# The end of a Strassen down product: its stores, its residual buffers and its early loads

## The chip, the cores and the metric

The kernel runs on one core of one Trainium2 chip. The metric is the device time in microseconds; three runs gave 2256.93 to 2257.66 us, median 2257.65 us.

## The reference, cut to what matters

A trunk of two layers on 1024 rows of width 1024, in float32. Layer 0 has an attention mixer, layer 1 a recurrent one. Each mixer and each FFN is a sub-layer with a norm ahead of it and one behind it:

```python
h = rmsnorm(x, norm_ffn_pre[layer])
f = (silu(h @ w_gate) * (h @ w_up)) @ w_down      # 1024 -> 2816 -> 1024
x = x + rmsnorm(f, norm_ffn_post[layer])
```

The part that is changed is the last product (`w_down`) and the residual addition behind it, once for each layer. Behind layer 0 the recurrent mixer follows, behind layer 1 the output.

## The kernel before, in words

Every matrix product is made in three passes on TensorE, high x high, high x low and low x high, so each float32 operand is split: a cast on ScalarE (line 584) and a subtraction on VectorE (line 585) give the two parts. The gate, up and down products are Strassen products with seven block products instead of eight.

`down` makes seven products out of 11 steps j each (2816 is 22 x 128, so a step j is a pair of row blocks of `w_down`). A step has 4 token blocks x 3 matmuls (lines 589 to 591, 128x128 by 128x512). The left operands (A11, S2, S3, S1, A22, S4, A12) were written to DRAM by the gate and up stage; the right operands are blocks of `w_down` or sums of them, kept in `t` tiles (one for each j, in a pool at the right end of the memory) until the fifth product. Each product's operands arrive through `raw` (three buffers), go through `split` into `w` (eight buffers, left) and `wb` (four buffers, right) and are used by TensorE in the order of j.

With the fifth product four of the eight row blocks are finished ("r = 1"), and `norm(1, a)` can be made for the four a: load x (line 181), multiply by the gain (line 212), square sum on ScalarE (line 164), rstd in one-column operations on GpSimd (lines 166 to 168), add (line 215), store (line 217, two DMAs of 64 rows each). Then come the sixth product (`p3`, left S4, loads at lines 681 and 682), which adds to the other four blocks, the eleven B21 blocks (line 691) and, one a after the other, the seventh product: three loads of A12 (through `load`, line 181), their splits (lines 700 and 701), 33 matmuls, the addition (line 706) and `norm(0, a)`. In layer 0 there is a `sink`: the norm goes on into the next mixer's norm (`pre_norm`, a second rstd and eight transposes on TensorE, line 197, whose results are split in lines 57 and 58). In layer 1 `sink` is None.

The order of each engine's instructions is set ahead of the run by a planner: it walks a timeline of its own and gives an engine next the first instruction in program order that this timeline finds ready. On the chip each engine, and each queue of DMA issues, then keeps that order and waits where something is late. `load` adds one rule: its DMA is issued behind the instruction `self.mark`, here the last load of the fifth product. All DMAs of this part are issued by SyncE, but for the second half of each store in layer 1, which ScalarE issues.

Of the kernel before, what the change touches and what calls it, by code (L numbers as in the profile page):

```python
# [8 lines left out]
F32 = mybir.dt.float32  # L9
# [6 lines left out]
P = 128  # L16
S = 1024
D = 1024
# [80 lines left out]
class Trunk:  # L99
# [98 lines left out]
            pst.append(ps.rearrange("p (a b) -> p a b", a=4))  # L198
        sink.take(t, pst, h, pool)

    def post_norm(self, ms, mg, x_src, x_dst, t, gpost, sink, pool):


        nc = self.nc
        x = pool.tile([P, D], F32, tag="nx", bufs=2, name=self.uid("x"))
        for d, s in rows(t, x_src):
            self.load(x[d, :], s)
        junk = pool.tile([P, D // len(ms)], BF16, tag="junk", bufs=1, name=self.uid("junk"))
        if mg is ms[0][1]:
            rs = self.rstd(pool, [m for _, m in ms], junk)  # L210
        for c, m in ms:
            nc.vector.tensor_tensor(mg[:, c], m, gpost[:, c], op=ALU.mult)
        if mg is not ms[0][1]:
            rs = self.rstd(pool, [m for _, m in ms], junk)
        nc.vector.scalar_tensor_tensor(x, mg, rs, x, op0=ALU.mult, op1=ALU.add)
        for k, (d, s) in enumerate(rows(t, x_dst)):
            (nc.scalar if k and sink is None else nc.sync).dma_start(s, x[d, :])
        if sink is not None:
            self.pre_norm(pool, x, mg, None, sink, t, self.psum_t)

# [187 lines left out]
    def out_product(self, ap, aT, w, x_src, x_dst, gpost_v, sink, kts):  # L408

        nc = self.nc  # L410
        wv = [w[kt * P:(kt + 1) * P, :].rearrange("p (a b) -> p a b", a=2) for kt in range(KT)]

        def act(kt, t0, n, pool, bufs, tag="act"):
            a = pool.tile([P, 384], F32, tag=tag, bufs=bufs, name=self.uid("act"))[:, :n * P]
            nc.sync.dma_start(a, aT[kt][:, t0 * P:(t0 + n) * P])
            return a

        def matmuls(ps, passes, first, last):

            for n in range(2):  # L420
                for i, (x, y) in enumerate(passes):
                    nc.tensor.matmul(ps[n], x, y[:, n, :], start=first and i == 0,
                                     stop=last and i == len(passes) - 1)

        def norm(t, ps):
            mg = ap.tile([P, D], F32, tag="mg", bufs=3, name=self.uid("mg"))
            ms = [(slice(i * 512, (i + 1) * 512), p) for i, p in enumerate(ps)]
            self.post_norm(ms, mg, x_src, x_dst, t, gpost, sink, ap)

        gpost = None  # L430
        for t0 in (0, 3):
            pst = [[self.psum() for _ in range(2)] for _ in range(3)]
            for kt in kts:
                pool, bufs = (self.apool, 1) if t0 == 0 and kt == kts[0] else (ap, 3)
                a = act(kt, t0, 3, pool, bufs)
                wh, wl = self.split(wv[kt], 2, 512)
                ah, al = (pool.tile([P, 384], F32R, tag=n, bufs=bufs, name=self.uid(n)) for n in ("ah", "al"))
                nc.scalar.copy(ah, a)
                nc.vector.tensor_tensor(al, a, ah.bitcast(F32), op=ALU.subtract)
                for t in range(3):  # L440
                    tok = slice(t * P, (t + 1) * P)
                    matmuls(pst[t], [(ah[:, tok], wh), (ah[:, tok], wl), (al[:, tok], wh)],
                            kt == kts[0], kt == kts[-1])
            if gpost is None:
                gpost = self.gain(ap, "gpost", gpost_v)
            for t in range(3):
                norm(t0 + t, pst[t])

        rows, acts = [], []
        for i, kt in enumerate(kts):  # L450
            raw = self.main.tile([P, 2, 512], F32, tag="w", bufs=8, name=self.uid("raw"))
            nc.sync.dma_start(raw, wv[kt])
            rows.append(raw)
            acts.append(act(kt, 6, 2, ap, 3, ("act", "ah", "al")[i % 3]))
        for t in range(2):
            ps = [self.psum() for _ in range(2)]
            for i in range(KT):
                matmuls(ps, [(acts[i][:, t * P:(t + 1) * P], rows[i])], i == 0, i == KT - 1)
            norm(6 + t, ps)
# [109 lines left out]
    def down(self, l, gO, x_src, x_dst, make_sink):  # L569
# [4 lines left out]
        nc, io = self.nc, self.io  # L574
# [4 lines left out]
        def block(j, row, c0=0, n=D):  # L579
            return w[(2 * j + row) * P:(2 * j + row + 1) * P, c0:c0 + n]  # L580
# [23 lines left out]
        with self.pool(f"d{l}") as ap:  # L604
# [3 lines left out]
            with self.pool(f"da{l}", "right") as da:  # L608
# [56 lines left out]
                    tt(n[:, hi], ps, n[:, lo], op=ALU.add)  # L665
                for n, ps in zip(m2, product(p4)):
                    tt(n[:, lo], n[:, lo], ps, op=ALU.subtract)
            with make_sink() as sink:
                def norm(r, a, m):
                    ms, mg = [(slice(0, D), m)], m  # L670
                    if r == 0 and sink is None:
                        ms = [(c, m[:, c]) for c in (hi, lo)]
                        mg = ap.tile([P, D], F32, tag="mg", bufs=1, name=self.uid("mg"))
                    self.post_norm(ms, mg, x_src, x_dst, (r, a), gpost, sink, ap)

                for a in range(4):
                    norm(1, a, m2[a])

                def p3(j):
                    r = main.tile([P, 2, 512], F32, tag="raw", bufs=3, name=self.uid("raw"))  # L680
                    nc.sync.dma_start(r[:, 0], gO["S4"][j])
                    nc.sync.dma_start(r[:, 1], block(j, 1, 512, 512))
                    return split(main, "w", 8, r[:, 0]), split(ap, "wb", 4, r[:, 1])

                for m, ps in zip(m1, product(p3)):
                    tt(m[:, hi], ps, m[:, hi], op=ALU.add)
                b21 = []
                for j in range(NP):
                    if j % 2 == 0:
                        r = main.tile([P, 2, 512], F32, tag="raw", bufs=3, name=self.uid("raw"))  # L690
                    nc.sync.dma_start(r[:, j % 2], block(j, 1, 0, 512))
                    b21.append(split(*((main, "w", 8) if j < 6 else (ap, "wc", 5)), r[:, j % 2]))
                for a in range(4):
                    ops = []
                    for j in range(0, NP, 4):
                        n = min(4, NP - j)
                        r = ap.tile([P, 4, P], F32, tag="act", bufs=2, name=self.uid("act"))[:, :n]
                        self.load(r, gO["A12"][:, j:j + n, a * P:(a + 1) * P])
                        t = ap.tile([P, 2, 4, P], F32R, tag="wb", bufs=4, name=self.uid("o"))
                        nc.scalar.copy(t[:, 0, :n], r)  # L700
                        tt(t[:, 1, :n], r, t[:, 0, :n].bitcast(F32), op=ALU.subtract)  # L701
                        ops += [(t[:, 0, i], t[:, 1, i]) for i in range(n)]
# [243 lines left out]
```

## Time and profile before

| | |
|---|---|
| median of the runs | 2257.65 us |
| profiled execution, own time | 2262.01 us |
| its span, first to last instruction | 2260.2 us |
| TensorE busy | 2201.2 us, 97% of the span |
| VectorE busy | 1551.9 us, 69% |
| ScalarE busy | 1149.1 us, 51% |
| GpSimd busy | 168.3 us, 7% |
| moved by DMA | 273.63 MB, mean 121 GB/s |

The shares are means over stages with different limits, so a change in one stage is read from that stage's own windows. In the rows PE is TensorE, PEld its weight loads, DVE VectorE, ACT ScalarE, POOL GpSimd and SP SyncE; a q behind the name is the engine's queue of DMA issues. `a <- b` behind a wait names what ended it. Times are microseconds from the first instruction.

### The profile page before, as it was taken

The numbers are of one execution on the slowest core, as the hardware profiler recorded it, in microseconds if no ns is written. First come the engines' busy times: TensorE is split into PE (matmuls) and PEld (weight loads), VectorE is DVE, ScalarE is ACT, GpSimd is POOL, SyncE is SP. The second block draws the span as 40 slices with busy tenths as digits, with TensorE's granted clock in tenths as the row PEclk, the third lists the DMA queues.
The fourth block names the chain that finished last, engine by engine and source line by source line (L and its number), as shares of the span: only waits on it lengthen the run. The fifth ranks groups of instructions, "written<-read, shape, count | busy, mean of one in ns | idle before, by whom it ended". The sixth has DMA issues, their size and how long they took to land. (4 is left out here: it accounts for less than half of the span.)

```text
span 2260.2 us, 30583 instructions
## 1 busy us (share of the span) xinstructions
PE 2201.2 (97%) x11136; PEld 1802.0 (80%) x11136; DVE 1551.9 (69%) x2514; ACT 1149.1 (51%) x2132; POOL 168.3 (7%) x370
## 2 busy tenths in 40 slices
PE   7999999999999999999999999999999999999997
PEld 6887888877678888888887777887788888888875
DVE  5676765464677767675866787536777767668665
ACT  4544455464665454532446567527755444424443
POOL 2111212131100000000001100001100000000010
PEclk9999999999999999999999999999999999999998
DMA  4101011124623333334558511358233333327466
GB/s 161 52 20 52 20 48 41 59 97 132 230 83 104 114 115 108 102 118 175 187 148 251 155 56 41 94 175 269 76 125 108 100 115 104 107 98 274 126 205 196
DMA packets 187271, 273.63 MB, mean 121 GB/s; under 512 B 13936, under 2 KB 115312, under 8 KB 187120
## 3 DMA queue, kind: packets, MB, share of 16 engines
q1 hardware_dynamic: 186480, 269.58, 38.0%
q10 hardware_dynamic: 640, 2.10, 0.3%
q8 instruction: 87, 1.43, 0.3%
q14 instruction: 64, 0.52, 0.1%
HBM read 206.09 MB, written 65.54 MB: 120 GB/s over the span
## 5 line engine op out<-in xcount | busy, mean ns | idle before, releaser
L509 PE MATMUL ps<-hS,q 128*128 128x512 f32 (+1 forms) x1288 | 490.9, 382 | 3.1 <-ACT hS L95 3.1
L510 PE MATMUL ps<-hS,q 128*128 128x512 f32 (+1 forms) x1288 | 490.9, 381 | 0.0
L511 PE MATMUL ps<-hS,q 128*128 128x512 f32 (+1 forms) x1288 | 489.9, 381 | 0.0
L490 DVE TENSOR_TENSOR q<-raw,q 128x512 fp32r<-128x512 f32 x308 | 204.7, 686 | 179.2 <-ACT q L489 178.7
L509 PEld LDWEIGHTS ps<-hS,q 128*128 128x128 f32 x1288 | 243.3, 189 | 50.2 <-ACT hS L95 3.9
L510 PEld LDWEIGHTS ps<-hS,q 128*128 128x128 f32 x1288 | 243.9, 189 | 46.7 <-DVE hS L88 0.4
L511 PEld LDWEIGHTS ps<-hS,q 128*128 128x128 f32 x1288 | 244.0, 189 | 45.8
L489 ACT CAST q<-raw 128x512 fp32r<-128x512 f32 x308 | 177.8, 616 | 168.8 <-DVE raw L498 130.4
L590 PE MATMUL ps<-o,o 128*128 128x512 f32 x616 | 240.9, 392 | 0.9 <-DVE o L585 0.8
L591 PE MATMUL ps<-o,o 128*128 128x512 f32 x616 | 238.2, 391 | 0.7 <-DVE o L701 0.7
L589 PE MATMUL ps<-o,o 128*128 128x512 f32 x616 | 221.1, 393 | 9.0 <-ACT o L700 5.5
L584 ACT CAST o<-raw 128x512 fp32r<-128x512 f32 x206 | 123.6, 620 | 193.8 <-PE ps L591 56.0
L478 ACT ACTIVATE raw<-raw,gcol 128x256 f32<-128x256 f32 x352 | 150.2, 498 | 139.0 <-DMA raw<-in_ffn_w_up_dram 71.8
L585 DVE TENSOR_TENSOR o<-raw,o 128x512 fp32r<-128x512 f32 x206 | 137.9, 688 | 66.4 <-ACT o L584 65.6
L589 PEld LDWEIGHTS ps<-o,o 128*128 128x128 f32 x616 | 115.7, 188 | 37.2 <-ACT o L700 7.7
L144 DVE TENSOR_TENSOR wlo<-raw,whi 128x1024 fp32r<-128x1024 f32 x76 | 93.4, 1230 | 66.0 <-ACT whi L143 65.1
L590 PEld LDWEIGHTS ps<-o,o 128*128 128x128 f32 x616 | 116.2, 189 | 26.6 <-DVE o L585 2.9
L591 PEld LDWEIGHTS ps<-o,o 128*128 128x128 f32 x616 | 116.1, 188 | 25.5 <-DVE o L701 1.6
L167 POOL TENSOR_SCALAR rs<-ss 128x1 f32<-128x1 f32 x64 | 31.8, 496 | 1270.2 <-ACT junk L164 1171.0
L143 ACT CAST whi<-raw 128x1024 fp32r<-128x1024 f32 x76 | 79.8, 1052 | 58.5 <-PE ps L155 24.7
L358 ACT COPY pt<-tr 128x512 f32<-128x512 f32 (+1 forms) x128 | 65.5, 527 | 78.5 <-PE tr L354 78.0
L154 PE MATMUL psq<-hT,whi 128*128 128x512 f32 x256 | 101.2, 395 | 1.1 <-DVE v L253 1.1
(185 smaller groups left out, 4237.6 us busy)
## 6 DMA issues: line engine op xcount, KB each, us to landing
raw<-in_ffn_w_down_dram SPq DMA_DIRECT2D x96, 256.0 KB, 4.6
raw<-in_ffn_w_gate_dram SPq DMA_DIRECT2D x44, 512.0 KB, 4.1
raw<-in_ffn_w_up_dram SPq DMA_DIRECT2D x44, 512.0 KB, 4.1
gS<-c SPq DMA_DIRECT2D x88, 256.0 KB, 3.6
raw<-gS SPq DMA_DIRECT2D x88, 256.0 KB, 3.0
gA<-c SPq DMA_DIRECT2D x66, 256.0 KB, 3.4
raw<-in_attn_w_in_dram SPq DMA_DIRECT2D x24, 512.0 KB, 3.9
raw<-in_attn_w_out_dram SPq DMA_DIRECT2D x24, 512.0 KB, 4.3
```

The lines of the kernel that those rows point to most:

```text
L154: nc.tensor.matmul(ps, wh[:, kt, cols], hh[:, kt, :], start=kt == 0, stop=False)
L478: nc.scalar.activation(raw[:, i], raw[:, i], AF.Copy, scale=gain[:, 4 * k + i:4 * k + i + 1])
L489: self.last = nc.scalar.copy(t[:, 0], src).ins
L490: nc.vector.tensor_tensor(t[:, 1], src, t[:, 0].bitcast(F32), op=ALU.subtract)
L509: nc.tensor.matmul(ps, a[:, 0, kt, :], bh, start=kt == 0, stop=False)
L510: nc.tensor.matmul(ps, a[:, 0, kt, :], bl, start=False, stop=False)
L511: nc.tensor.matmul(ps, a[:, 1, kt, :], bh, start=False, stop=kt == 3)
L584: nc.scalar.copy(t[:, 0], src)
L585: tt(t[:, 1], src, t[:, 0].bitcast(F32), op=ALU.subtract)
L589: nc.tensor.matmul(ps, a[0], b[:, 0], start=first, stop=False)
L590: nc.tensor.matmul(ps, a[0], b[:, 1], start=False, stop=False)
L591: nc.tensor.matmul(ps, a[1], b[:, 0], start=False, stop=last)
```

## The change

Four things, all in `down` and in `post_norm`, which it calls:

- The stores of the finished rows are issued by GpSimd in both layers. Only the very last row block, (0, 3) of layer 1, keeps SyncE and ScalarE. (`out_product`, which calls `post_norm` too, names SyncE as before.)
- In layer 1 a new pool `late`, in the memory that the `t` tiles leave, holds six residual buffers (`nx`), six A12 buffers and six B21 buffers of two blocks each. In layer 0 there are three residual buffers instead of two, and A12 and B21 keep their buffers.
- `norm(1, j)` is issued inside the sixth product, behind the loads and splits of step j, for j = 0 to 3. `self.mark` moves on with each S4 load, so a `load` goes behind the S4 load of its step.
- In layer 1, steps 4 to 9 of the sixth product also issue the eleven B21 loads, two a step, and steps 6 and 8 the three A12 loads of a = 0 and a = 1. The splits of B21 stay behind the sixth product in program order.

```diff
+    def post_norm(self, ms, mg, x_src, x_dst, t, gpost, sink, pool, store, x_pool=None, n_x=2):
-        x = pool.tile([P, D], F32, tag="nx", bufs=2, name=self.uid("x"))
+        x = (x_pool or pool).tile([P, D], F32, tag="nx", bufs=n_x, name=self.uid("x"))
...
-            (nc.scalar if k and sink is None else nc.sync).dma_start(s, x[d, :])
+            store[k].dma_start(s, x[d, :])
...
+                late = es.enter_context(self.pool("late", "right")) if sink is None else None
...
-                    self.post_norm(ms, mg, x_src, x_dst, (r, a), gpost, sink, ap)
-
-                for a in range(4):
-                    norm(1, a, m2[a])
+                    last = late and (r, a) == (0, 3)
+                    self.post_norm(ms, mg, x_src, x_dst, (r, a), gpost, sink, ap,
+                                   [nc.sync, nc.scalar] if last else [nc.gpsimd] * 2, late, 6 if late else 3)
+
+                def rows_of(a):
+                    rs = []
+                    for j in range(0, NP, 4):
+                        n = min(4, NP - j)
+                        r = (late or ap).tile([P, 4, P], F32, tag="act", bufs=6 if late else 2,
+                                              name=self.uid("act"))[:, :n]
+                        self.load(r, gO["A12"][:, j:j + n, a * P:(a + 1) * P])
+                        rs.append((n, r))
+                    return rs
+
+                def b21_load(j):
+                    if j % 2 == 0:
+                        r = late.tile([P, 2, 512], F32, tag="b21", bufs=6, name=self.uid("raw")) if late else (
+                            main.tile([P, 2, 512], F32, tag="raw", bufs=3, name=self.uid("raw")))
+                    else:
+                        r = b21[-1][0]
+                    self.load(r[:, j % 2], block(j, 1, 0, 512))
+                    return r
...
                 def p3(j):
                     r = main.tile([P, 2, 512], F32, tag="raw", bufs=3, name=self.uid("raw"))
-                    nc.sync.dma_start(r[:, 0], gO["S4"][j])
+                    self.mark = nc.sync.dma_start(r[:, 0], gO["S4"][j]).ins
                     nc.sync.dma_start(r[:, 1], block(j, 1, 512, 512))
-                    return split(main, "w", 8, r[:, 0]), split(ap, "wb", 4, r[:, 1])
+                    o = split(main, "w", 8, r[:, 0]), split(ap, "wb", 4, r[:, 1])
+                    if j < 4:
+                        norm(1, j, m2[j])
+                    elif late:
+                        b21.extend((b21_load(i), i % 2) for i in range(2 * j - 8, min(2 * j - 6, NP)))
+                        if j in (6, 8):
+                            early.append(rows_of(j // 2 - 3))
+                    return o
...
+                for j in range(len(b21), NP):
+                    b21.append((b21_load(j), j % 2))
+                b21 = [split(*((main, "w", 8) if j < 6 else (ap, "wc", 5)), r[:, i])
+                       for j, (r, i) in enumerate(b21)]
                 for a in range(4):
                     ops = []
-                    for j in range(0, NP, 4):
-                        n = min(4, NP - j)
-                        r = ap.tile([P, 4, P], F32, tag="act", bufs=2, name=self.uid("act"))[:, :n]
-                        self.load(r, gO["A12"][:, j:j + n, a * P:(a + 1) * P])
+                    for n, r in early[a] if a < len(early) else rows_of(a):
```

## Rows read from the trace of the kernel before

**Rows 1.** Windows, layer 1: length, each engine's busy us (x count), clock, DMA share, GB/s

```profile
2162.00:2181.60 19.60, 19.60 (x88) 16.25 (x87) 11.32 (x18) 7.85 (x14) 0.00 (x0) 1.00 0.89 269
2181.60:2194.40 12.80, 12.59 (x56) 10.10 (x55) 11.23 (x13) 7.10 (x13) 8.15 (x8) 1.00 0.45 112
2194.40:2220.00 25.60, 20.24 (x82) 14.61 (x80) 16.23 (x24) 10.82 (x20) 0.00 (x0) 0.96 1.02 308
2220.00:2231.00 11.00, 10.61 (x38) 8.62 (x39) 5.35 (x8) 5.19 (x9) 0.00 (x0) 0.79 0.57 175
2231.00:2250.30 19.30, 19.27 (x86) 15.62 (x84) 12.46 (x17) 6.93 (x17) 3.74 (x9) 1.00 0.59 157
```

**Rows 2.** Waits of TensorE, 2175 to 2261 us: total us, times, longest

```profile
PE ps L589 <- ACT o L700: 3.2, 1, 3.2
```

**Rows 3.** Waits of SyncE's queue, 2160 to 2261 us

```profile
SPq L217 <- DVE x L215: 17.5, 6, 6.9
SPq L181 <- DMA out_dram<-x: 9.8, 5, 4.0
SPq L681 <- DVE o L585: 8.4, 7, 3.6
```

**Rows 4.** Timeline of SyncE's queue: start, length, line, what is moved

```profile
2162.07 2.39 SPq L181 DMA_DIRECT2D x<-xs  x4
2164.55 0.53 SPq L681 DMA_DIRECT2D raw<-gS  x1
...
2181.30 0.43 SPq L682 DMA_DIRECT2D raw<-in_ffn_w_down_dram  x1
2188.68 0.51 SPq L217 DMA_DIRECT2D out_dram<-x  x1
...
2194.36 0.71 SPq L681 DMA_DIRECT2D raw<-gS  x1
...
2204.96 1.58 SPq L691 DMA_DIRECT2D raw<-in_ffn_w_down_dram  x2
```

**Rows 5.** Timeline of VectorE: the last read of a `t` tile

```profile
2165.27 0.69 DVE L653 TENSOR_TENSOR raw<-t,raw 128x512 f32<-128x512 f32 x1 [1.16 <-DMA raw<-in_ffn_w_down_dram]
```

**Rows 6.** Windows, layer 0, columns as in rows 1

```profile
1202.00:1220.00 18.00, 18.00 (x85) 14.85 (x83) 12.75 (x17) 13.00 (x23) 7.33 (x10) 1.00 0.69 208
1220.00:1240.00 20.00, 17.40 (x81) 13.07 (x81) 16.26 (x25) 16.37 (x31) 3.71 (x6) 1.00 1.00 304
1240.00:1260.00 20.00, 16.82 (x71) 12.28 (x70) 16.82 (x23) 7.79 (x13) 1.77 (x2) 1.00 0.73 193
1260.00:1280.00 20.00, 18.17 (x84) 13.80 (x83) 15.57 (x19) 16.04 (x25) 6.66 (x12) 1.00 0.85 233
```

**Rows 7.** Waits of SyncE's queue, 1180 to 1300 us

```profile
SPq L217 <- DVE x L215: 13.1, 4, 6.6
...
SPq L181 <- DMA xs<-x: 4.4, 5, 2.2
```

**Rows 8.** Waits of TensorE, 1180 to 1300 us

```profile
PE pst L197 <- DVE hT L58: 2.5, 3, 1.3
PE ps L589 <- ACT o L700: 2.3, 2, 1.7
```

**Rows 9.** Timeline after 2249 us, TensorE's last matmul and the last addition

```profile
2249.88 0.39 PE L591 MATMUL ps<-o,o 128*128 128x512 f32 x1
...
2251.13 0.68 DVE L706 TENSOR_TENSOR m<-ps,m 128x512 f32<-128x512 f32 x1
```

**Rows 10.** Timeline of ScalarE: a square sum (layer 0), a store's issue (layer 1)

```profile
1207.77 1.06 ACT L164 ACTIVATE m<-x 128x1024 f32<-128x1024 f32 x1 [2.16 <-DVE x L215]
1208.73 0.18 ACT L164 ACTIVATION_READ_ACCUMULATOR m<-x 128x1 f32 x1
...
2188.69 0.56 ACTq L217 DMA_DIRECT2D out_dram<-x  x1
```

**Rows 11.** Timeline of GpSimd: an rstd operation in layer 1

```profile
2183.55 1.46 POOL L168 TENSOR_TENSOR rs<-rs,neghalf 128x1 f32<-128x1 f32 x1
```

More of the change, by code (lines that the diff above doesn't have):

```diff
@@ L199, in pre_norm @@
         sink.take(t, pst, h, pool)
-    def post_norm(self, ms, mg, x_src, x_dst, t, gpost, sink, pool):
+    def post_norm(self, ms, mg, x_src, x_dst, t, gpost, sink, pool, store, x_pool=None, n_x=2):
         nc = self.nc
-        x = pool.tile([P, D], F32, tag="nx", bufs=2, name=self.uid("x"))
+        x = (x_pool or pool).tile([P, D], F32, tag="nx", bufs=n_x, name=self.uid("x"))
         for d, s in rows(t, x_src):
@@ L427, in norm @@
             ms = [(slice(i * 512, (i + 1) * 512), p) for i, p in enumerate(ps)]
-            self.post_norm(ms, mg, x_src, x_dst, t, gpost, sink, ap)
+            self.post_norm(ms, mg, x_src, x_dst, t, gpost, sink, ap, [nc.sync])
         gpost = None
@@ L667, in down @@
                     tt(n[:, lo], n[:, lo], ps, op=ALU.subtract)
-            with make_sink() as sink:
+            with ExitStack() as es:
+                sink = es.enter_context(make_sink())
+                late = es.enter_context(self.pool("late", "right")) if sink is None else None
                 def norm(r, a, m):
@@ L679, in p3 @@
+                def b21_load(j):
[6 more added lines that the diff above has]
+                    return r
+                early, b21 = [], []
                 def p3(j):
@@ L685, in down @@
+                    return o
                 for m, ps in zip(m1, product(p3)):
                     tt(m[:, hi], ps, m[:, hi], op=ALU.add)
[L687 to L692, printed above, removed]
+                for j in range(len(b21), NP):
+                    b21.append((b21_load(j), j % 2))
```

## The prediction

> **What bounds the kernel now.** The groups were read in this order: first how busy TensorE is over the end of the second down product, then what it waits for, then what holds back the queue that feeds it, then the same for the first down product. TensorE is the bound nearly everywhere, so only stretches where it loses time can pay. In the second FFN's end it runs at its undisturbed rate until 2181.6 us: 88 matmuls in 19.6 us, 4.49 per us [rows 1]. From 2181.6 to 2231 us (49.4 us) it does 56 + 82 + 38 = 176 where that rate gives 222; the missing 46 are 10.2 us. After 2231 us it is undisturbed again (86 in 19.3 us). Of the 10.2 us, 0.21 + 5.36 + 0.39 = 6.0 us are idle (length less busy time in the same rows); the other 4.2 us are matmuls at the lower level of the clock, 1.2 instead of 2.4 GHz: the granted clock reads 0.96 and 0.79 there, against 1.00 in the rows around, and it falls behind the idle stretch. So an idle microsecond here costs more than one.
>
> The longest single idle time is the last product waiting for its A12 operand, 3.2 us, which is a late load [rows 2]. The reader is to see why in the SyncE queue [rows 3, 4]: after the load of 2181.30 us its next instruction is a store of the finished rows at 2188.68 us, and the next S4 load goes out at 2194.36 us. The B21 loads start only at 2204.96 us. In that hole the DMA engines are at 0.45 and 112 GB/s; just before they are at 0.89 and 269, just after at 1.02 and 308 GB/s [rows 1]. The queue stood 17.5 us for the normalised rows that its stores need and 9.8 us for stores to land whose residual buffer a new load reuses; 8.4 us it stood for a free `raw` buffer, which stays [rows 3].
>
> In the first FFN the end of the down product has the same form: TensorE is idle 2.60 + 3.18 + 1.83 = 7.6 us between 1220 and 1280 us [rows 6]; the queue stands 13.1 us for stores and 4.4 us for residual buffers [rows 7].
>
> **The change part by part, second FFN.** (1) Fourteen of the sixteen stores leave SyncE and ScalarE for GpSimd, and six buffers take the reuse wait away. The hole from 2181.6 to 2194.4 us fills. At 308 instead of 112 GB/s it can take 12.8 x 196 = 2.5 MB more, which is 8.1 us at 308 GB/s. The bytes that were through by 2220.0 us are then through by about 2211.9 us. (2) B21 (eleven loads of 256 KB) and six of the twelve A12 loads go out beside the sixth product. They add no bytes; the second unit's A12, 0.72 MB, comes forward, 2.3 us at that rate, but stands behind what the first unit needs. (3) TensorE itself: from 2181.6 us the rest of the sixth product would end near 2211 us (132 matmuls at 4.49 per us are 29.4 us). So the transfers become just fast enough and no more. (4) VectorE is the other near bound: it was busy 11.23 + 16.23 = 27.5 us in the 38.4 us to 2220.0 us [rows 1], and that work must now fit into some 30 us in an order that was fixed beforehand. With both at over nine tenths I do not take the whole 10.2 us as gain. What must be left is at least the 0.9 us by which the transfers end after the product (2211.9 against 2211); at most, with the transfers no better than before, 10.2 us. I take 3.7 us as left: 1 us for the transfers, some 1.5 us for VectorE, 1.2 us for the clock falling behind an idle stretch again, in the ratio of the rows above (4.2 to 6.0). **Gain 6.5 us.**
>
> (5) New loads use memory of the released `t` tiles, so the first residual load waits until those are read; the last such read starts at 2165.27 us [rows 5]. The first S4 load goes out at 2164.55 us, ahead of the residuals instead of behind their four issues (2162.07 us) [rows 4]. Behind a blocked residual load stand the next S4 loads, by 1.4 us at most; nothing waits for these before 2181 us, so I cost it at nothing. (6) The last row block keeps its stores on SyncE and ScalarE. After TensorE's last matmul (2249.88 us) the last add starts only at 2251.13 us, behind the block before it [rows 9]; with A12 there earlier that block is done sooner, and the 1.25 us can shrink to what a matmul's end needs. Bounds 0 and 0.8 us, taken: **gain 0.4 us**. The rest of the tail stays.
>
> **First FFN.** Stores move to GpSimd, three residual buffers instead of two, and each norm is issued behind an S4 load of its own, for the first four units. A12 keeps two buffers and B21 is loaded where it was, so the A12 waits (2.3 us [rows 8]) stay. The stretch at 208 GB/s before 1220 us can move 18 x 96 = 1.7 MB more, 5.7 us at 304 GB/s [rows 6]; that covers the 2.60 us idle up to 1240 us and a part of the next 3.18. I take 3.5 us for it; the bounds are 0 (the planned order moves the idle time elsewhere) and 5.3 (7.6 less the A12 waits).
>
> Against it stands the price on GpSimd, which has no DMA in the trace. A store's issue on ScalarE took 0.56 us, the longest one-column operation on GpSimd 1.46 us [rows 10, 11]; a pair is bounded by 1.1 and 2.9 us, and I take 2.0 us, the middle, since it is a transfer's issue on the engine of the second row. Behind the pair on GpSimd stands the rstd of the same rows; the square sum it needs takes 1.06 + 0.18 us on ScalarE [rows 10] from the same instant, so the delay is 2.0 - 1.25 = 0.75 us for each of eight norms, and the transposes on TensorE wait for its result. Transposes waited 2.5 us in all for what lies ahead of them [rows 8], so most delays have cover; two exposed ones make 1.5 us. **Net gain 2.0 us** (3.5 - 1.5). In the second FFN no transpose follows a norm, and the pair costs nothing there: even the last rstd, with the pair of the third row block ahead of it, comes a whole unit of 33 matmuls later (33 at 4.49 per us, 7.3 us); without that cover it would be up to 2.9 us at the end.
>
> **Sum.** 6.5 + 0.4 + 2.0 = 8.9 us. The profiled execution's own time is 2262.0 us (span 2260.2 and 1.8 around it), so it would be 2253.1 us; it was 4.4 us above the median of the runs, 2257.65 us, and the forecast for a median is 2257.65 - 8.9 = 2248.8 us, own range 2245 to 2252.5.
>
> **Two rules weighed.** The trace has DMA engines at a share of 1.02 just where the new loads would land [rows 1]. The Trainium skill (DMA: Bandwidth & Descriptors, Issuing engines are not separate DMA queues) says that transfers started by different engines run on the same 16 DMA engines and that spreading them saves only the issuing sequencer's time. By that rule alone the sum would be sixteen issues of about half a microsecond less the next limit; the queue's stands of 17.5 and 9.8 us [rows 3] show that more than issue time is in it here, though the shared engines are the first rival below.
>
> GpSimd's one-column operation took 1.46 us here [rows 11] while VectorE was at work. The Trainium skill (SBUF — State Buffer, Who interferes with whom) says that a VectorE operation with two SBUF inputs holds off a GpSimd operation that reads SBUF, and that descriptors of a GpSimd DMA starve only beside VectorE's two-port modes. By that rule the stores would not be held off by the adds and multiplies here; no row of before shows a GpSimd DMA. The third rival does not rest on it.
>
> **Rivals.** *Shared DMA engines.* B21 and A12 share one queue with S4 and stand ahead of the last S4 loads: 2.9 + 1.4 MB are 14 us at 308 GB/s. If the sixth product's last operands come later for it, TensorE idles there instead, the clock falls once more, and 8 us of the 10.2 stay. Gain 2.2 + 0.4 + 1 = 3.6: 2254 us. For it: 1.02. Against it: the filled hole.
>
> *The change does not do what it says.* The planned order keeps the queue standing for `raw` buffers (8.4 us [rows 3]) and puts other waits into the hole: gain about 1, 2256.6 us. Against it: the longest stands are for stores and their buffers, which are gone.
>
> *GpSimd becomes the bound, slower.* If a pair of stores takes 4 us, every rstd behind it in the first FFN comes 2.75 us late, and with transposes waiting each time 8 x 2.75 = 22 us come against 10.4: 2269 us. It decides for slower from 8 x (p - 1.25) = 10.4 + 4.5, p = 3.1 us, above the upper bound taken from the rows.
>
> *All fits.* Only 1.1 of the 10.2 us stay and the first FFN gains 4: 9.1 + 0.4 + 4 = 13.5, 2244.1 us.
>
> **How the numbers follow.** Chances: forecast 0.50, shared engines 0.21, nothing done 0.09, GpSimd bound 0.08, all fits 0.12. The time is the forecast's. The range takes in all but GpSimd and the far ends of the others: 2243 to 2257. What a measurement of this kernel can tell from no change is about 0.2%, 4.5 us. Below 2253.1 us lie all fits, nearly all of the forecast and half of the shared-engine case: 0.71. Slower than 2262.2: most of the GpSimd case and a little for an order planned badly, 0.09. The rest is 0.20.
>
> **What would show it.** Right: SyncE without a stand for stores, DMA share near 1 from the first B21 load on, TensorE at 1.00 clock through the last product, its wait for A12 gone, GpSimd stores of about 1 us each. Wrong: casts that wait for S4 late in the sixth product (shared engines), GpSimd ahead of the transposes' waits (third rival), or a second FFN that still loses over 7 us.

## The result and the profile after: slower by half a per cent

Four runs of the changed kernel gave 2268.05 to 2271.08 us, median 2270.41, against 2257.65 for the kernel before (four runs). The ratio on record is 1.0047, 95% interval 1.0035 to 1.0059; the two medians alone give 12.8 us, 1.0057. Forecast were 2248.8 us, so the sign is wrong. The profiled execution took 2269.78 us, 7.8 more than that of before.

Where the 7.8 us are, from the starts of same-numbered matmuls in the two traces (from the first matmul of each product to the first of the next, in layer 0's and layer 1's seventh to the start of the last; worked out):

| stretch | before | after | change |
|---|---|---|---|
| ahead of layer 0's sixth product | 1198.1 | 1195.2 | -2.9 |
| layer 0, sixth + seventh product | 35.7 + 39.8 | 41.3 + 41.0 | +6.8 |
| from there to layer 1's sixth product | 906.5 | 906.6 | +0.1 |
| layer 1, sixth product | 32.6 | 45.1 | +12.5 |
| layer 1, seventh product | 37.2 | 29.7 | -7.5 |
| last matmul to the end | 10.3 | 9.2 | -1.1 |

The first line lies ahead of the change; over the traces of this case, whose code is the same up to there, it reads 1193.8 to 1199.3. The seventh product and the tail gained even more than forecast; the sixth products of both layers lost more than that.

**Layer 1.** Windows of the kernel after, columns as in [rows 1]:

```profile
2166.00:2184.00 18.00, 18.00 (x81) 14.92 (x80) 7.61 (x12) 5.50 (x9) 0.00 (x0) 1.00 0.99 241
2184.00:2190.00 6.00, 5.76 (x23) 3.87 (x22) 2.69 (x5) 2.62 (x5) 0.00 (x0) 1.00 1.04 278
2190.00:2200.00 10.00, 7.13 (x30) 5.47 (x30) 10.00 (x12) 6.97 (x13) 6.70 (x8) 1.00 0.79 265
2200.00:2220.00 20.00, 16.30 (x56) 12.57 (x56) 10.40 (x15) 5.78 (x10) 4.53 (x9) 0.83 0.96 312
2220.00:2229.00 9.00, 5.83 (x24) 4.46 (x25) 8.18 (x14) 6.73 (x13) 0.00 (x0) 1.00 0.81 233
2229.00:2259.00 30.00, 30.00 (x134) 24.66 (x132) 18.38 (x27) 10.25 (x23) 6.72 (x15) 1.00 0.36 96
```

The hole in the DMA share did fill: 1.04 and 0.79 where 0.45 stood [rows 1]. But TensorE is idle 2.87 of 10 us beside it, and behind that the clock is at 0.83. What filled the hole is seen in the timeline of SyncE's queue (start, length, line, what):

```profile
2178.45 1.63 SPq L181 DMA_DIRECT2D x<-xs  x2
2180.56 0.33 SPq L708 DMA_DIRECT2D raw<-gS  x1
...
2183.11 1.47 SPq L181 DMA_DIRECT2D raw<-in_ffn_w_down_dram  x2
2187.16 0.33 SPq L708 DMA_DIRECT2D raw<-gS  x1
...
2191.85 2.98 SPq L181 DMA_DIRECT2D act<-gA  x3
2201.05 0.33 SPq L708 DMA_DIRECT2D raw<-gS  x1
```

Residual rows, B21 and A12 went out, and the S4 load at 2201.05 us, the eighth, is the one that went out at 2194.36 us before [rows 4]. Counted from the product's first matmul that is 17.0 us where it was 14.3: 2.8 us later, beside the 3.9 us by which the whole product starts later. The queue's waits (2160 to 2270 us) and TensorE's say why; columns as in [rows 2, 3]:

```profile
SPq L708 <- DVE o L586: 11.5, 6, 5.9
SPq L181 <- DVE o L731: 8.8, 4, 4.4
```

```profile
PE ps L590 <- ACT o L585: 5.8, 3, 2.7
PE ps L591 <- DVE o L586: 2.8, 1, 2.8
PE ps L590 <- DVE m L668: 1.2, 1, 1.2
```

L708 is the S4 load, and `o L586` the subtraction in `split` that frees its `raw` buffer. The stand of 8.4 us [rows 3] that was to stay is now 11.5, and it comes behind residual, B21 and A12 loads instead of stores. VectorE, which has to free the buffer, is busy 10.00 of 10 us there. The A12 wait of before [rows 2] is gone and the seventh product runs at 1.00.

The tail, TensorE's last matmul and the addition behind it, which now waits for nothing else (its start is 0.42 us behind that matmul's, instead of the 1.25 of [rows 9]):

```profile
2258.82 0.39 PE L592 MATMUL ps<-o,o 128*128 128x512 f32 x1
```

```profile
2259.24 0.69 DVE L736 TENSOR_TENSOR m<-ps,m 128x512 f32<-128x512 f32 x1 [2.71 <-PE ps L592]
```

**Layer 0.** Windows, SyncE's longest stand for a store, TensorE's longest wait, the answers to [rows 6 to 8]:

```profile
1202.00:1220.00 18.00, 16.50 (x77) 13.40 (x75) 10.38 (x13) 9.31 (x16) 8.94 (x14) 1.00 0.60 171
1220.00:1240.00 20.00, 15.86 (x69) 13.37 (x70) 16.45 (x24) 16.96 (x31) 8.82 (x10) 0.83 1.00 295
```

```profile
SPq L181 <- DMA xs<-x: 7.3, 3, 4.5
```

```profile
PE pst L197 <- DVE hT L58: 5.6, 1, 5.6
```

The stretch before 1220 us moves 171 GB/s, less than the 208 of before: with three buffers and each norm behind an S4 load, the fourth block's residual load still waits for the first block's store to land (4.5 us), and three S4 steps stand behind it (1212.88 to 1216.60 us). ScalarE's cast of the first of these loads comes late, and behind its subtraction stands, on VectorE, the split that the transposes wait for:

```profile
1219.43 0.62 ACT L585 CAST o<-raw 128x512 fp32r<-128x512 f32 x1 [5.76 <-DMA raw<-gS]
1223.40 1.28 DVE L58 TENSOR_TENSOR hT<-pst,hT 128x512 fp32r<-128x512 f32 x2
```

Transposes wait 5.6 us in one piece, and the clock reads 0.83. The queue's stands for `raw` grew here too, from 7.0 to 14.3 us between 1180 and 1300 us; no run gives layer 0's S4 loads buffers of their own, so what these stands cost there is not shown.

GpSimd's issue is cheap; its timeline in layer 1:

```profile
2241.38 1.17 POOL L218 DMA_DIRECT2D out_dram<-x  x2 [1.62 <-DVE x L216]
```

1.17 us for a pair, where 2.0 were taken; SyncE takes 1.10 for a pair of layer 0 in e10 below.

### The profile page after: what moved, and what is told of

Read it like the earlier page. It is cut to its first block, busy times and chain, and to the rows that moved or that the text cites. A ratio compares the mean times of both kernels' runs of the same rounds, so it can differ in the third digit from the quotient of the medians.

```text
span 2268.0 us, 30584 instructions
## 1 busy us (share of the span) xinstructions
PE 2204.1 (97%) x11136; PEld 1804.2 (80%) x11136; DVE 1551.6 (68%) x2514; ACT 1148.6 (51%) x2132; POOL 186.9 (8%) x400
## 5 line engine op out<-in xcount | busy, mean ns | idle before, releaser
L586 DVE TENSOR_TENSOR o<-raw,o 128x512 fp32r<-128x512 f32 x206 | 137.7, 687 | 84.0 <-ACT o L585 82.9
L590 PEld LDWEIGHTS ps<-o,o 128*128 128x128 f32 x616 | 116.7, 190 | 39.2 <-ACT o L585 9.5
```

What stands on the lines that cost most here:

```text
L586: tt(t[:, 1], src, t[:, 0].bitcast(F32), op=ALU.subtract)
L590: nc.tensor.matmul(ps, a[0], b[:, 0], start=first, stop=False)
```

## Experiments

Times are medians, ratios are to the kernel before on the same chip. The expectations name theories by letters: A the early loads, B the norms inside the steps, C or G GpSimd, V the splits on VectorE that free `raw` late. The columns behind are from one profiled run each: layer 0's sixth and seventh product and the way from there to layer 1's first (together 828.6 to 830.4 us in e9 to e12 and g1, the five kernels that leave layer 0 alone, 831.0 in the kernel before), and layer 1's sixth and seventh.

| | us | before | ratio (95%) | layer 0: 6th + 7th, way | layer 1: 6th + 7th |
|---|---|---|---|---|---|
| e1 | 2271.02 | 2259.52 | 1.0054 (1.0042-1.0067) | 37.3 + 38.6, 763.4 | 36.2 + 36.1 |
| e2 | 2268.23 | 2259.52 | 1.0036 (1.0024-1.0048) | 39.2 + 41.0, 754.5 | 39.1 + 35.2 |
| e3 | 2266.97 | 2259.52 | 1.0035 (1.0023-1.0047) | 40.7 + 39.0, 755.4 | 43.0 + 29.7 |
| e4 | 2265.70 | 2259.52 | 1.0025 (1.0014-1.0036) | 38.6 + 40.2, 755.9 | 38.4 + 33.9 |
| e5 | 2273.13 | 2260.22 | 1.0056 (1.0044-1.0068) | 35.1 + 41.0, 764.1 | 43.6 + 29.7 |
| e6 | 2265.62 | 2260.22 | 1.0025 (1.0017-1.0034) | 36.8 + 41.4, 755.8 | 38.5 + 34.7 |
| e7 | 2271.60 | 2260.22 | 1.0050 (1.0038-1.0062) | 30.7 + 50.6, 756.2 | 40.7 + 33.5 |
| e8 | 2259.79 | 2260.22 | 1.0000 (0.9992-1.0009) | 37.2 + 40.2, 756.0 | 32.4 + 34.9 |
| e9 | 2263.82 | 2259.31 | 1.0017 (1.0008-1.0025) | 34.1 + 40.1, 756.2 | 49.5 + 30.0 |
| e10 | 2248.91 | 2259.31 | 0.9953 (0.9941-0.9965) | 33.6 + 39.7, 756.2 | 34.4 + 29.7 |
| e11 | 2252.58 | 2259.31 | 0.9964 (0.9952-0.9976) | 33.1 + 40.6, 756.0 | 34.2 + 29.7 |
| e12 | 2252.21 | 2259.31 | 0.9970 (0.9959-0.9981) | 34.3 + 38.9, 756.3 | 30.6 + 33.6 |
| f1 | 2258.81 | 2259.18 | 0.9992 (0.9982-1.0002) | 41.3 + 40.8, 756.1 | 32.2 + 29.7 |
| f2 | 2261.18 | 2259.18 | 1.0007 (0.9998-1.0016) | 38.1 + 37.8, 763.7 | 34.6 + 29.7 |
| f3 | 2260.80 | 2259.18 | 1.0005 (0.9996-1.0014) | 39.9 + 37.0, 764.1 | 34.0 + 29.7 |
| f4 | 2249.45 | 2259.18 | 0.9955 (0.9941-0.9969) | 35.5 + 40.7, 757.2 | 32.1 + 29.7 |
| f5 | 2256.31 | 2259.59 | 0.9984 (0.9972-0.9995) | 39.9 + 39.8, 755.5 | 32.5 + 30.1 |
| g1 | 2247.22 | 2259.59 | 0.9945 (0.9931-0.9958) | 33.4 + 39.5, 755.7 | 29.9 + 29.7 |

A column counts from the first matmul of a product to the first of the next, so a wait ahead of the seventh product stands in the sixth's. In layer 1 that is a wait for A12 in four kernels: 5.2 us in e2, 3.5 in e4, 4.5 in e6, 10.6 in e7. From first to last matmul their sixth product takes 33.5, 34.5, 33.6 and 29.7 us; for the kernel before it is 32.4, for the kernel after 44.8.

All the kernels below share one more thing with the kernel after: B21's loads stand ahead of B21's splits in program order, where the kernel before mixes them, and go through `load`. No run tests this alone. In layer 0 of the five kernels that have nothing else, the traces are 0.6 to 2.4 us shorter than that of the kernel before.

### One part at a time (e1 to e5)

e1 is the kernel before with one edit:

```diff
-            (nc.scalar if k and sink is None else nc.sync).dma_start(s, x[d, :])
+            store[k].dma_start(s, x[d, :])   # nc.gpsimd, but for (0, 3) of layer 1
```

> The kernel before with one part of the change: stores issued by GpSimd (but the last row block of layer 1), in both layers. Theory A (the early B21 and A12 loads displace S4): the stores are harmless; SyncE no longer stands for them, the sixth product of layer 1 takes 30 to 31 us instead of 32.6, that of layer 0 33 to 35 instead of 35.7; time 2252 to 2256 us. Theory B (norms and their residual loads inside the steps of the sixth product): the same, as they are ahead of it here. Theory C (GpSimd stores themselves are the cost, by the rstd behind them and by slow landing that holds residual buffers): slower than before, 2262 us or more, the sixth product of layer 0 near 41 us.

e2 is the changed kernel without the early loads, e3 the changed kernel with the norms ahead of the sixth product again, e4 both:

```diff
-                        b21.extend((b21_load(i), i % 2) for i in range(...))     # e2, e4
-                        if j in (6, 8):
-                            early.append(rows_of(j // 2 - 3))
...
-                    if j < 4:                                                    # e3, e4
-                        norm(1, j, m2[j])
+                for a in range(4):                                   # ahead of product(p3)
+                    norm(1, a, m2[a])
```

> The changed kernel without the early loads: B21 and A12 of layer 1 are loaded behind the sixth product's loads, into the same larger buffers. Theory A: the sixth product of layer 1 falls from 45.1 to about 33 us, the last product rises from 29.7 to some 33 us; time about 2262 us; layer 0 unchanged (41.3 us). Theory B: the residual loads are still between the S4 loads, so the sixth product of layer 1 stays above 40 us and the time at 2268 us or more. Theory C: no change, 2270 us.

> The changed kernel with the four norms of finished rows put ahead of the sixth product again, in both layers, the early loads and all buffers kept. Theory A: layer 1 stays at 43 to 45 us for the sixth product, layer 0 gets back to about 36; time 2266 us. Theory B: the sixth product of layer 1 falls to 35 us or less and that of layer 0 to 35, time 2254 us. Theory C: 2270 us.

> The changed kernel with both undone: norms ahead of the sixth product and no early loads; GpSimd stores, the larger buffers and the mark that moves with S4 stay. Theory A and B: sixth product of layer 1 at 30 to 33 us, of layer 0 at 34 to 36; time 2250 to 2256 us. Theory C: 2265 us or more.

e5 is the changed kernel with its stores back on SyncE and ScalarE:

```diff
-                                   [nc.sync, nc.scalar] if last else [nc.gpsimd] * 2, ...)
+                                   [nc.sync, nc.scalar if sink is None else nc.sync], ...)
```

> The changed kernel with its stores back on SyncE (layer 0) and on SyncE and ScalarE (layer 1); early loads, norms inside the steps and all buffers stay. Theory G (GpSimd is the cost: its stores go out behind the rstd work of the next rows, some 3 us late, and a residual load waits for their landing): layer 0 loses at most 1 us against before instead of 6.4, time 2262 us or less. Theory V (the splits that free the raw buffers stand behind the norms on VectorE, and the new loads and norms between the S4 loads make that worse): SyncE stands for the stores again, the sixth product of layer 1 stays at 43 us or more, layer 0 at 40; time 2270 us or more.

Each part explains some and none all. Early loads cost layer 1's sixth product, first to last matmul, 8.3 to 11.3 us (44.8 in the kernel after against 33.5 in e2, 42.8 in e3 against 34.5 in e4), and what comes behind it, the wait for A12 and the seventh product, is shorter by 7.9 to 10.9: next to nothing in sum. Norms inside the steps cost layer 1 about 2 us in sum. GpSimd alone (e1) loses as much as the whole change, 8 us of it on the way to layer 1 (763.4; see layer 0 below). Yet taking GpSimd away (e5) brings nothing back: layer 0's sixth product is short again (35.1), as theory G had it, but the way is 764.1 and layer 1 stays at 43.6. So the store's engine isn't the cause by itself. The telling one is e4: stores off SyncE, six residual buffers, nothing early, and the sixth product takes 34.5 us where 32.4 stood before, with 3.5 us of waiting for A12 behind it. Its window and SyncE's longest stand:

```profile
2184.00:2194.00 10.00, 7.51 (x32) 5.47 (x30) 10.00 (x13) 6.05 (x11) 6.93 (x11) 1.00 0.24 74
```

```profile
SPq L714 <- DVE o L587: 15.2, 7, 10.4
```

The hole that the change was to fill is there again, at 0.24, with no store on the queue. Its end is the eighth S4 load at 2194.05 us, 15.0 us behind the product's first matmul (14.3 before). It waits for a `raw` buffer; the split that frees it stands on VectorE behind the norms, which now come together (10.00 of 10 us busy).

### Is it the place of the norms on VectorE, or the buffers? (e6 to e8)

e6 and e7 are e4 with the norms elsewhere, e8 is e4 with buffers of its own for layer 1's sixth product (four residual buffers and three for B21 make room):

```diff
+                    if j in (1, 3, 5, 7):             # e6; in e7 all four behind product(p3)
+                        norm(1, j // 2, m2[j // 2])
...
-                    r = main.tile([P, 2, 512], F32, tag="raw", bufs=3, ...)
+                    r = late.tile([P, 2, 512], F32, tag="s4", bufs=6, ...)    # e8, layer 1
```

> As e4 (no early loads, GpSimd stores, larger buffers), but the four norms of finished rows are issued in steps 1, 3, 5 and 7 of the sixth product, in both layers, so that VectorE has splits between them. Theory V: the sixth product of layer 1 takes 31 to 33 us instead of e4's 38.4, that of layer 0 35; time 2256 to 2261 us. Theory G: the stores and rstd are the same, so nothing is gained against e4: 2264 to 2267 us.

> As e4, but the four norms stand behind the whole sixth product in program order, in both layers. Theory V: the sixth product of layer 1 comes to 30 to 31 us, with the S4 load of step 7 issued within 4 us of the one of step 6 instead of 11; the norms then load VectorE in the last product, which takes 31 to 36 us; time 2252 to 2260 us. Theory G: the sixth product stays at 36 us or more.

> As e4, but in layer 1 the sixth product's operands come into six buffers of their own instead of the three raw buffers (with four residual buffers and three for B21, to fit). Theory V: loads no longer wait for the splits, so the wait for late S4 loads goes, but the splits still stand behind the norms; sixth product of layer 1 33 to 35 us; time 2258 to 2263 us. Theory G: 38 us as in e4, 2265 us.

It is both. With the norms spread (e6) little changes: the longest stand for `raw` is 10.8 us. With the norms behind (e7) the sixth product takes 29.7 us, as theory V expected, in layer 0 as in layer 1, on three `raw` buffers and with a hole in the DMA share (0.47 from 2187 to 2201 us):

```profile
2187.00:2217.00 30.00, 29.99 (x133) 24.51 (x131) 20.43 (x25) 12.22 (x22) 10.36 (x16) 1.00 0.76 218
```

But the eight residual loads then go out from 2200.37 us on, ahead of B21, and A12 only from 2219.19 us, so that the seventh product waits and the time is 2271.60 us, not the 2252 to 2260 expected:

```profile
PE ps L592 <- ACT o L743: 10.6, 1, 10.6
```

So the `raw` ring is short because the norms stand ahead of the splits on VectorE, and the empty stretch of the DMA engines cost nothing there by itself. Buffers help without that price: e8's sixth product takes 32.2 us instead of 34.5, and the wait for A12 behind it is gone, though the queue still stands 10.2 us in one piece for a buffer.

### Both ends of that (e9 to e12)

e9 is layer 0 as before and layer 1 as changed. The other three keep layer 0 as before. e10 is e8's layer 1 with nine S4 buffers, B21 through `raw`, and A12 of two units loaded behind the last S4 load. e11 is e10 with stores on SyncE and ScalarE. e12 is the kernel before with S4 buffers of its own in layer 1, in the new pool; the two residual and the two A12 buffers lie there too, and `raw` is left to B21:

```diff
-                    r = main.tile([P, 2, 512], F32, tag="raw", bufs=3, ...)
+                    r = late.tile([P, 2, 512], F32, tag="s4", bufs=9, ...)    # e12: 6
...
+                        if j == NP - 1:                                       # e10, e11
+                            early.extend(rows_of(a) for a in (0, 1))
```

> Layer 0's down product exactly as in the kernel before; layer 1's with the whole change. Theory: the loss has two places, some 6 us at the end of layer 0's product and the start of the recurrent mixer, some 4 us in layer 1. Then layer 0 is back at the kernel before and the time is about 2262 us (+4). Rival, all of the loss comes from layer 1: about 2270. Rival, all of it from layer 0: about 2258. In every case layer 1's sixth product takes about 45 us and the seventh about 30, since nothing changes there.

> Layer 0 as before. Layer 1: norms ahead of the sixth product, stores from GpSimd, four residual buffers, the sixth product's operands in nine own buffers instead of the three of raw, B21 through raw as before, A12 of the first two units loaded behind the last S4 load. Theory (the queue stood for raw buffers that the splits free, and the early loads cost only where they stand ahead of S4): the sixth product near 31 us (32.6 before), the seventh near 31 (37.2 before), tail 9.2: about 2250 us (-7). Rival (VectorE, full with norms and splits in 2185 to 2200, sets the sixth product itself): the sixth product stays at 35 us or more, time 2256 to 2259. Rival (A12 ahead of B21 only moves the wait): the sixth 32, a wait of 3 us or more for B21's splits in the seventh, 2256.

> As e10, but the stores stay on SyncE and ScalarE. If the queue's stands for the stores matter once raw buffers are no longer scarce: the last S4 loads stand behind stores, the sixth product takes 35 us or more and the time is 4 us or more above e10's. If only raw buffers mattered: within 2 us of e10.

> The kernel before with one change: the sixth product of layer 1 reads its operands through six buffers of its own in the memory of the t tiles, not through the three of raw (the residual buffers lie there too, still two). Stores on SyncE and ScalarE, no early loads. If raw buffers alone set the hole before 2194 us: sixth product 30 us (-2.6), 2254 to 2255 us. If the stand for stores sets it, as the prediction had it: sixth product unchanged at 32 to 33 us, within 1.5 us of the kernel before.

e12 decides between the stores and the buffers. The stores still stand on SyncE (16.9 us in all), and the kernel is 0.30% faster (0.19 to 0.41). Its window over the old hole:

```profile
2181.00:2194.00 13.00, 12.57 (x56) 10.10 (x55) 10.94 (x14) 5.84 (x11) 4.46 (x5) 1.00 0.93 268
```

0.93 and 268 GB/s where 0.45 and 112 stood [rows 1]. Ten of the eleven S4 loads are out by 2180.01 us, ahead of the first store; and since B21 no longer shares `raw` with S4, six B21 loads are out by 2178.3 us, where the first went out at 2204.96 before. So the seventh product gains more (3.6 us) than the sixth (2.0). e1, which has the same order of the B21 loads and three `raw` buffers, kept the hole: SyncE stood 10.6 us in one piece for `raw` there.

e10 has early A12 where nothing needed stands behind it, GpSimd's stores, nine S4 buffers and four residual ones, and is 0.47% faster; its sixth product takes 34.4 us, not the 31 expected. e11's stores on SyncE cost 3.7 us by the medians (the intervals overlap), between its two expectations, and its trace shows none of it in layer 1 (34.2 + 29.7 against 34.4 + 29.7). The Trainium skill's rule that another issuing engine saves only the sequencer's time (DMA: Bandwidth & Descriptors, Issuing engines are not separate DMA queues) agrees with that: in layer 1 the stores' engine moved little, the buffers much. e9 splits the loss: +4.5 us from layer 1, so some 8 of the 12.8 by the medians from layer 0 (6.8 in the traces).

### Layer 0 (f1 to f5), and what is left in layer 1 (g1)

All six have e10's layer 1. In f1 to f5 layer 0 differs:

```diff
# f1: as the changed kernel          f2: stores from GpSimd, nx bufs=2, norms ahead
# f3: f2 with nx bufs=3              f4: f3 with stores on SyncE
-                    nc.sync.dma_start(r[:, 0], gO["S4"][j])               # f5: f3 and
+                    self.mark = nc.sync.dma_start(r[:, 0], gO["S4"][j]).ins
# g1: e10 with two residual buffers in layer 1 instead of four
```

> Layer 1 as in e10 (2248.9 us there); layer 0's down product with the whole change: stores from GpSimd, three residual buffers, norms inside the steps. If layer 0 costs what the difference of the changed kernel and e9 says, some 6 us: 2255. Rival, layer 0 costs nothing of its own and the loss came from layer 1 alone: within 2 us of e10.

> As e10; in layer 0 only the stores move to GpSimd, two residual buffers, norms ahead. Theory P (a store from GpSimd goes out behind rstds on that engine and lands later, so that the next residual load, which reuses its buffer, is late and the S4 and A12 loads stand behind it on SyncE): the dearest of the four, 8 us above e10, 2257. Rival I (only the order of norms inside the steps costs): within 2 us of e10.

> As f2 with a third residual buffer. Theory P: the reuse comes one block later, so half or more of f2's loss is gone: 2250 to 2253. Rival I: within 2 us of e10. If GpSimd's part of the price is the rstd behind the pair of stores, as the prediction had it, the third buffer does not help and it is as f2.

> As e10; in layer 0 only a third residual buffer, stores on SyncE, norms ahead. Prediction's view (the reuse wait of 4.4 us holds the queue): 1 to 3 us below e10, 2246 to 2248. Rival (the queue then stands for the stores or for raw in the same place): within 2 us of e10.

> As f3 (layer 0: stores from GpSimd, three residual buffers, norms ahead), but self.mark moves on with each S4 load of layer 0 as in the changed kernel, so that x and A12 loads are planned behind the S4 load before them. The stores, their number, engine and buffers are those of f3; only the planned order differs. If the price in layer 0 is GpSimd's own (issue time, landing time): as f3, about 2260. If it is the order (three transposes planned ahead of matmuls that are ready, one idle stretch of 3.5 to 5.7 us and the clock falling behind it): that stretch is not there (first product of the recurrent mixer some 756 us ahead of layer 1's down product, not 764) and the time is within 5 us of e10 and f4, 2249 to 2254.

> As e10, but two residual buffers in layer 1, so that only two of the four x loads (1 MB instead of 2 MB) stand ahead of the first S4 loads, as in e12. Expected: the S4 loads go out at e12's times, the sixth product takes 31 to 32 us instead of 34.4, the seventh stays near 30: 2 to 3 us below e10, 2246 to 2247. Rival (the later x loads then wait for stores to land and hold B21 behind them): the seventh product takes 33 us or more and the time is that of e10 or above.

f1 is 9.9 us above e10, more than the 6 expected for layer 0. f1 to f4 ran on one chip: f3 and f4 differ in the stores' engine alone, by 11.4 us. The third buffer is worth nothing either way (f3 against f2, f4 against e10). Theory P, by which it would take back half of the loss, fell, and theory I as well. GpSimd's own time is no cause either: in f3 the rstd behind a pair of stores starts 0.10 to 0.55 us after the end of its square sum, in e10, without the pair, 0.09; over eight norms the pairs make 1.5 us, not 11. What f2 has, beside a wait of 3.6 us in its sixth product, is one idle stretch at the start of the recurrent mixer:

```profile
1280.61 1.08 PE L199 MATMUL pst<-ident,m 128*128 128x128 f32 x4 [3.48 <-DVE hT L60]
```

The transposes before it were done at 1275.92 us, and VectorE's split of them (L60) comes only at 1279.77. VectorE's timeline in f2 shows why: gain and split of the mixer's weights (L141, L146) and an addition (L747) stand ahead of it in the planned order.

```profile
1275.77 1.23 DVE L141 TENSOR_TENSOR raw<-raw,gcol 128x1024 f32<-128x1024 f32 x1 [0.20 <-DMA raw<-in_rg_w_in_dram]
1276.91 1.22 DVE L146 TENSOR_TENSOR wlo<-raw,whi 128x1024 fp32r<-128x1024 f32 x1
1278.04 0.69 DVE L747 TENSOR_TENSOR m<-ps,m 128x512 f32<-128x512 f32 x1
1278.64 1.22 DVE L141 TENSOR_TENSOR raw<-raw,gcol 128x1024 f32<-128x1024 f32 x1
1279.77 1.28 DVE L60 TENSOR_TENSOR hT<-pst,hT 128x512 fp32r<-128x512 f32 x2
```

In e10 the two splits lie between these, and TensorE waits 1.23 us at most:

```profile
1269.42 1.22 DVE L141 TENSOR_TENSOR raw<-raw,gcol 128x1024 f32<-128x1024 f32 x1
1270.57 0.68 DVE L60 TENSOR_TENSOR hT<-pst,hT 128x512 fp32r<-128x512 f32 x1
1271.17 1.22 DVE L146 TENSOR_TENSOR wlo<-raw,whi 128x1024 fp32r<-128x1024 f32 x1
1272.30 0.68 DVE L747 TENSOR_TENSOR m<-ps,m 128x512 f32<-128x512 f32 x1
1272.90 0.68 DVE L60 TENSOR_TENSOR hT<-pst,hT 128x512 fp32r<-128x512 f32 x1
```

The clock in 1275 to 1285 us is 0.69 in f2 and 1.00 in e10. A single idle stretch (3.5 to 5.7 us) at this place is in e1, e5, f2 and f3, and these four have a way of 763 to 764 us; all others have 754 to 757. e5's stores are on SyncE, and the same five instructions stand on VectorE there, up to their order; its stretch ends with ScalarE's scaling of the next rows, 0.07 us behind the split. So the stretch comes from an order that is planned anew, and GpSimd's stores are not needed for it.

f5 shows it from the other side: f3's stores, another order, and the way is 755.5 again. But only 4.5 of the 11.4 us come back by the medians, fewer than expected (f5's eleven runs lie between 2250.55 and 2263.88 us). The sixth product takes 39.9 us as in f3, where f4's takes 35.5, and has the changed kernel's wait:

```profile
PE pst L199 <- DVE hT L60: 4.5, 1, 4.5
```

There SyncE stands 4.7 us for a store to land, with S4 loads behind it, as in the changed kernel. So the two places of layer 0's loss are shown, and the order as the cause of the second. The cause of the first is read from the traces alone; whether there is an order in which stores from GpSimd cost nothing was not tried.

g1 came as expected. With two residual loads instead of four ahead of them, the last S4 load goes out at 2175.82 us (2180.30 in e10), and the sixth product loses nothing. The two buffers also hold back the norms: the third addition of a norm comes at 2196.88 us, in e10 at 2192.24, and the one wait of TensorE in e10's sixth product (2.5 us) is for a split on VectorE. The runs do not part the two. g1's windows:

```profile
2174.00:2190.00 16.00, 16.00 (x73) 13.24 (x72) 15.95 (x22) 11.34 (x20) 7.91 (x12) 1.00 1.08 348
2190.00:2206.00 16.00, 16.00 (x72) 13.28 (x71) 11.20 (x17) 7.72 (x14) 2.16 (x4) 1.00 0.94 275
```

2247.22 us, 0.55% faster than before (0.42 to 0.69), is the best of all: layer 0 untouched, the sixth product's loads free of `raw`, A12 behind them.

## Why the prediction was wrong

- **Step (1), "The hole from 2181.6 to 2194.4 us fills": this step failed.** It took the longest stand of the queue (17.5 us, stores) for the cause and put the 8.4 us for `raw` aside as "which stays". They stood in the same place, and the shorter one was enough to keep the hole: with the stores gone it grew to 15.2 us (e4), and with the buffers free the hole filled beside the stores (e12). In the kernel after the hole's share did fill, but with residual, B21 and A12 loads; the S4 loads behind `raw` came later, and the term "gain 6.5 us" became a loss (3.9 us of layer 1 in the traces, tail included; 4.5 by the medians of e9). Nor was the hole what cost TensorE its time: in e7 it stood open beside a product without idle time. The rival "does not do what it says" named the stand; it was priced at a gain of 1 us.
- **Step (2), "stands behind what the first unit needs".** It does, but ahead of the last S4 loads. This is the shared-engines rival's mechanism, on the queue rather than in the DMA engines: 8.3 to 11.3 us more in the sixth product (against e4 and e2). The gain in the seventh, 7.5 us, is real and stays when the loads go out behind S4 (29.7 in e10 and g1).
- **Steps (3) and (4), "just fast enough"; VectorE's 27.5 us in 30.** g1 does the sixth product in 29.9 us with VectorE at 15.95 of 16 us and no idle of TensorE; 33 matmuls for each of four blocks at 4.49 per us are 29.4. So the 3.7 us taken as left were too many; layer 1 could have gained 2.7 + 7.5 + 1.1 = 11.3 us in the profiled runs.
- **Step (5)**, the wait for the `t` tiles, cost nothing: the first residual load follows the first S4 step on the queue without a gap (2167.22 us). **Step (6)**, the tail, gained 1.1 where 0.4 was taken and 0.8 was the bound; the last addition's wait went as described.
- **First FFN, "Net gain 2.0 us": wrong in sign**, 7 to 10 us lost (6.8 in the traces of before and after, 9.9 from e10 to f1). The price per pair was over-estimated (1.17 against 2.0), and it delays an rstd by 0.5 us at most. The step that failed is the lower bound of 0, where "the planned order moves the idle time elsewhere": a new order makes waits of its own. f1, f2, f3 and f5 each have a single wait of 3.5 to 5.8 us, the clock reads 0.74, 0.69, 0.66 and 0.84 in the 10 us behind or around it, and they lie 7 to 12 us above f4. The chance of "an order planned badly" was named, as a small part of 0.09.
- The slower rival, **GpSimd as the bound** from p = 3.1 us, named the right sign for a wrong reason.

## What to carry to other kernels

When several waits hold one queue in the same stretch, ask for each what the queue would do if the others were gone; the change that helps takes away the one that then still binds, here a three-buffer ring that is freed late, and a kernel with that edit alone, everything else standing, finds it (e12). A load that is brought forward on a first-in-first-out queue is free only behind everything that is needed earlier. Where the order is planned ahead, moving even a 0.5 us instruction to another engine reorders the others: what that costs is read from the new order, not from the instruction's price.

## What was not expected of the hardware

- Store issue on GpSimd is hardly dearer than on SyncE: a pair of stores of 64 x 1024 float32 takes 1.09 to 1.34 us on GpSimd (e10, layer 1) and 1.10 to 1.23 us on SyncE (e10, layer 0).
- The clock and the idle time did not go together simply. f5 idles 4.5 us in one wait, and 1225 to 1235 us stand at 0.84; e10 idles 2.5 us in one wait, and 2190 to 2200 us stand at 0.83; e6 idles 3.4 us in one wait at 1220.6 us and reads 1.00 from 1215 to 1245 us. What tells them apart the runs do not settle.
- The DMA share of 1.08 at 348 GB/s in g1, beside TensorE at 1.00 and VectorE at 15.95 of 16 us, was more than the 308 GB/s at 1.02 of [rows 1], without an idle of TensorE.
